# Layer 0's mixer of a two-layer hybrid network: small products put in another order, a low-rank factor split 80 + 80

## The chip, the cores and the metric

The kernel runs on one core of a Trainium2 chip. The metric is the device time of one execution in microseconds (us), the median of several runs. It is a forward pass of two layers over 256 tokens of width 2048, batch 1.

## The reference

Each layer is a mixer, a residual with a layer norm, a feed-forward block with a short convolution, and another residual with a layer norm. Layer 0's mixer, which the change touches, projects the tokens with one matrix, gives half of the columns to stick-breaking attention and the other half to a recurrence of 16 heads of 64:

```
rw = token_shift(rw, shift_mu)
r, kr, vr, dw, da, dg = split_last(rw, [1024, 1024, 1024, 64, 64, 160])
w_log = -softplus(-(w0 + tanh(dw) @ w2)) - 0.5
decay = exp(-exp(w_log))
a = sigmoid(a0 + da @ a2)
g = sigmoid(dg) @ g2                       # rank 160
kk = (k * k_k) per head, divided by its norm
k = k * (1 + (a - 1) * k_a)
state = state * w_t + (state @ -kk_t) (kk_t a_t)^T + v_t k_t^T     # per token and head
y = state @ r_t
out = (group_norm(y) + bonus) * g
```

Layer 1's mixer is gated linear attention; it is not touched.

## The kernel before, in words

**The large products.** All weights stream from HBM once. A *granule* is 128 x 512 weights in float32; ScalarE copies it into a rounded float32r part (L56), VectorE forms the remainder (L57), and TensorE makes three products for each operand pair, high by high, high by low and low by high (L185 to L187 for feature tiles, 12 products of 256 columns a granule; L195 to L197 for token tiles). These products take most of the time.

**What sets the order.** TensorE's order is the order in which the program is written; the other engines are ordered by a scheduler. Work beside the large products is written as generators (`spawn`): each `yield n` lets n granules pass (`tick`), then its next step is written into the stream. The names below are such generators of `Mix0.run`.

- `lora` (L588 and on): the low-rank steps. For each of 8 pairs of heads it makes two products, L601 for the decay (rows 0 to 63 of the low-rank input) and L602 for `a` (rows 64 to 127), of 256 columns in float32. ScalarE applies a sigmoid to each result (L157), VectorE sums the decays within chunks (L611). Pairs 0 to 3 are written in one batch, then a granule, then pairs 4 to 7, then a granule. Then ScalarE changes its table (L148) and raises the sums to exponents, two for each pair (L157, with a copy, L625). A granule later come the products of the gate, L634 with the first 128 of the 160 rows of `g2` and L635 with the last 32, four pairs, a granule, four pairs; VectorE copies them out (L636). `lw`, `g2a` and `g2b` lie in the three buffers through which the weights also arrive.
- `k_post` and `r_post`: for each pair the norm of the keys (L665 and ScalarE's logarithm and exponents), the scaled keys and queries (`BK` in `PB`, and `AR`, L678 to L690), and then the **Gram products**, L697: keys against queries for each of the 4 chunks of 64 tokens and each of the 2 heads. A head lies in 64 of the 128 partitions, so each product has 64 rows. The four chunks of the first head come first, then those of the second; each head has its own PSUM tile `pg`.
- `chain`: the recurrence over 4 chunks, for all 16 heads, in four steps a chunk that lie 4 granules apart: L809 (`pu`), L819 (`psa`), then L828 (`pS_`, the new state) and directly behind it the output `py`. `py` is the sum of two products per head: L840 from `SV` and `Gr` (128 rows, 64 columns of output) and, from chunk 1 on, L842 from the old state `So` and `AR` (64 rows). The two are written in turn, head by head: 16 + 16 products a chunk. `epilogue` then normalizes `py`.

A float32 product of the program shows as two MATMUL records, each with a weight load. The records name the shape: `128*64` is 128 rows by 64 output columns of the array, and `64x64` the partitions and columns of what streams.

PSUM tiles of these generators come from one pool of four (`t`).

Of the kernel before, what the change touches and what calls it, by code (L numbers as in the profile page):

```python
# [10 lines left out]
P = 128  # L11
S = 256
# [6 lines left out]
# how many granules the steps of the work beside the products lie apart  # L19
# [3 lines left out]
class Stream:  # L23
    """Weight granules [128, 512] in the order of use, split into two float32r parts."""
# [7 lines left out]
    def ahead(self):  # L32
        """split the first four granules before those of the stream before have been used"""
        K = self.K
        K.wpos = 0
        self.ready = [self.make() for _ in K.wbase]
# [27 lines left out]
class Kern:  # L64
# [14 lines left out]
    # Work beside the products: a generator that yields the number of granules to let pass  # L79
    # before its next step.  # L80
# [40 lines left out]
    def wpools(self, ctx, n, nraw, nw):  # L121
        """weights arrive n granules at a time"""
# [5 lines left out]
    def wextra(self, ctx, n, start=0):  # L128
        """room for n more granules as long as ctx is open"""
# [6 lines left out]
    def rsqrt(self, x, y, t):  # L136
        """y = x^-1/2 by exp(-ln(x)/2) and one step of Newton; t is scratch"""
        nc = self.nc
# [6 lines left out]
    # The table sets of ScalarE are loaded where act_set says: what needs a table is issued  # L145
    # behind its load, and a load behind what needs the set before it.
# [23 lines left out]
    def split(self, dst, src, eng_hi="act"):  # L170
        """dst [128, 2, n] float32r <- src in two parts"""
        nc = self.nc
# [6 lines left out]
    # out[f, tok] += W[k, f] x[k, tok]; a granule holds 4 k tiles of one feature tile  # L179
# [10 lines left out]
    # out[tok, n] += x[k, tok] W[k, n], both in two float32r parts; a granule holds 512 columns  # L190
    # of one k tile
# [7 lines left out]
    # out[tok, n] += x[k, tok] W[k, n]; a granule holds 512 columns of one k tile  # L199
    def wave(self, st, xT, made=None, first=False):  # L200
        """four feature tiles at once, k outside; made: steps that give 2 k tiles each"""
# [45 lines left out]
    def block_a(self, st, xs):  # L247
        """512 columns, both halves of the tokens"""
# [9 lines left out]
    def proj_out(self, xs, st, done, then=None, tail=4, after=None):  # L258
        """xs: (high, low) halves per k tile and token half; done(m, nb, ps, columns)"""
        nc = self.nc  # L260
        n = len(xs)
        for nb in range(4):
# [5 lines left out]
            # the first half of the tokens ends ahead of the second, and that in two parts  # L268
# [64 lines left out]
    def norm_out(self, h, g_d, b_d, out):  # L333
        """the last norm: a job before the sums are complete, that gives what follows each half"""
# [4 lines left out]
        # the blocks of each half that ScalarE and GpSimd take  # L339
# [164 lines left out]
C = 64  # L504
# [26 lines left out]
class Mix0:  # L531
# [19 lines left out]
    def run(self, xT, made, win_b, win_v, win_qk, lw_d, g2_d, open_h, outer):  # L551
# [6 lines left out]
        with ExitStack() as ctx:  # L558
# [28 lines left out]
            def lora(ps):  # L587
# [10 lines left out]
                for p in range(NP):  # L598
# [15 lines left out]
                    if p == 3:  # L614
                        yield 1
# [787 lines left out]
```

## Time and profile before

| | |
|---|---|
| median of three runs | 2439.29 us (2438.54 to 2439.73) |
| span of the profiled execution, first to last instruction | 2437.5 us |
| TensorE busy | 2405.3 us (99%) |
| VectorE busy | 1554.8 us (64%) |
| ScalarE busy | 1301.8 us (53%) |
| read from HBM | 429.77 MB, 177 GB/s over the span |
| mean granted TensorE clock | 0.991 |

The profiled execution's own time is its span, 2437.5 us; the median of the runs is 1.8 us above it, 0.07%. How to read a timeline row: start in us, length in us, engine, source line, operation, tiles written and read, shape, number of records merged, and in brackets the idle time of the engine ahead of it with what ended it. The lengths of TensorE's records overlap, so the time that a block takes is read from its first start to the start of what follows.

### The profile page before, as it was taken

The page shows a single profiled execution, that of the slowest core. Times are in us where ns is not written, and L with a number is a line of the kernel's source. Part 1 is how long each engine was busy: PE and PEld are TensorE (multiplying, and loading weights), DVE is VectorE, ACT ScalarE, POOL GpSimd, SP SyncE. Part 2 cuts the span into 40 slices and gives each one's busy share as a digit, 9 for nine tenths or more (in the row PEclk, how much of TensorE's full clock was granted, in tenths as well). Part 3 has the DMA queues.
Part 4 walks back from the last instruction along what each step waited for, and adds up shares of the span by engine and source line. Part 5 has one row for each costly group of instructions (what it writes and reads, how often), then busy time and mean ns, then how long its engine had stood idle before and what let it go on. Part 6 is the DMA issues. An engine that isn't in the chain of part 4 may idle for free.

```text
span 2437.5 us, 44745 instructions
## 1 busy us (share of the span) xinstructions
PE 2405.3 (99%) x17770; PEld 2253.8 (92%) x17770; DVE 1554.8 (64%) x2847; ACT 1301.8 (53%) x2450; POOL 12.0 (0%) x14
## 2 busy tenths in 40 slices
PE   8999999999999999999999999999999999999997
PEld 7998988889999999988898998989999999998887
DVE  5887755677666666655558666667766666655555
ACT  6655555555555555544437555555555555554442
POOL 0000000000000000000000000000000000000001
PEclk9999998999999999999999999999999999999999
DMA  5444433656555555555555554564655555565553
GB/s 175 161 134 168 145 105 104 210 163 224 189 184 185 188 183 188 184 193 195 184 173 177 170 173 166 175 213 163 218 184 189 183 185 188 183 216 199 195 186 138
DMA packets 123698, 434.79 MB, mean 178 GB/s; under 512 B 13744, under 2 KB 14640, under 8 KB 123488
## 3 DMA queue, kind: packets, MB, share of 16 engines
q1 hardware_dynamic: 123488, 431.93, 52.7%
q8 instruction: 139, 2.28, 0.4%
q14 instruction: 71, 0.58, 0.1%
HBM read 429.77 MB, written 2.10 MB: 177 GB/s over the span
## 4 chain that ended last, share of the span: by engine, by line
PE 95%; DVE 3%; DMA 1%; ACT 1%; issue 0%; SPq 0%; DVEq 0%; ACTq 0%
PE g L185 17%; PE g L187 17%; PE g L186 17%; PE g L195 10%; PE g L196 10%; PE g L197 10%; PE t L197 1%; PE t L195 1%; PE t L196 1%; DMA raw<-w0b 1%; PE g L213 1%; PE g L216 1%; PE g L214 1%; PE t L185 1%; PE t L187 1%; PE t L186 1%
## 5 line engine op out<-in xcount | busy, mean ns | idle before, releaser
L57 DVE TENSOR_TENSOR w<-raw,w 128x512 fp32r<-128x512 f32 x1584 | 1080.1, 690 | 769.9 <-ACT w L56 766.4
L56 ACT CAST w<-raw 128x512 fp32r<-128x512 f32 x1584 | 965.6, 620 | 958.3 <-PE g L187 461.4
L185 PE MATMUL g<-x,w 128*128 128x256 f32 x3024 | 852.6, 282 | 0.0
L187 PE MATMUL g<-x,w 128*128 128x256 f32 x3024 | 852.1, 282 | 0.0
L186 PE MATMUL g<-x,w 128*128 128x256 f32 x3024 | 851.8, 282 | 0.0
L185 PEld LDWEIGHTS g<-x,w 128*128 128x128 f32 x3024 | 569.7, 188 | 0.2
L186 PEld LDWEIGHTS g<-x,w 128*128 128x128 f32 x3024 | 569.7, 188 | 0.3
L187 PEld LDWEIGHTS g<-x,w 128*128 128x128 f32 x3024 | 569.6, 188 | 0.0
L197 PE MATMUL g<-w,hT 128*128 128x512 f32 (+1 forms) x704 | 255.4, 363 | 0.0
L196 PE MATMUL g<-w,hT 128*128 128x512 f32 (+1 forms) x704 | 255.3, 363 | 0.0
L195 PE MATMUL g<-w,hT 128*128 128x512 f32 (+1 forms) x704 | 255.3, 363 | 0.0
L185 PE MATMUL g<-xi,w 128*128 128x256 f32 x608 | 179.2, 295 | 0.0
L187 PE MATMUL g<-xi,w 128*128 128x256 f32 x608 | 173.4, 285 | 3.0 <-DVE w L57 2.9
L186 PE MATMUL g<-xi,w 128*128 128x256 f32 x608 | 172.8, 284 | 0.0
L195 PEld LDWEIGHTS g<-w,hT 128*128 128x128 f32 x704 | 133.0, 189 | 20.7
L196 PEld LDWEIGHTS g<-w,hT 128*128 128x128 f32 x704 | 133.0, 189 | 20.5
L197 PEld LDWEIGHTS g<-w,hT 128*128 128x128 f32 x704 | 132.9, 189 | 20.5
L187 PEld LDWEIGHTS g<-xi,w 128*128 128x128 f32 x608 | 116.1, 191 | 3.8 <-DVE w L57 3.8
L185 PEld LDWEIGHTS g<-xi,w 128*128 128x128 f32 x608 | 116.2, 191 | 3.1 <-issue 1.5
L186 PEld LDWEIGHTS g<-xi,w 128*128 128x128 f32 x608 | 116.3, 191 | 0.8
L213 PE MATMUL g<-x,w 128*128 128x256 f32 x192 | 55.8, 298 | 0.0
L157 ACT ACTIVATE ct<-ct 128x256 f32<-128x256 f32 x88 | 36.8, 418 | 32.5 <-DVE ct L457 32.5
(316 smaller groups left out, 2852.2 us busy)
## 6 DMA issues: line engine op xcount, KB each, us to landing
raw<-up SPq DMA_DIRECT2D x352, 512.0 KB, 3.6
raw<-dn SPq DMA_DIRECT2D x176, 512.0 KB, 4.3
raw<-w0b SPq DMA_DIRECT2D x53, 512.0 KB, 3.6
raw<-w1b SPq DMA_DIRECT2D x40, 512.0 KB, 3.8
raw<-w0qk SPq DMA_DIRECT2D x32, 512.0 KB, 3.6
raw<-w0o SPq DMA_DIRECT2D x32, 512.0 KB, 4.2
raw<-w1v SPq DMA_DIRECT2D x32, 512.0 KB, 3.6
raw<-w1o SPq DMA_DIRECT2D x32, 512.0 KB, 4.4
```

The costliest lines, as they stand in the source:

```text
L56: i = nc.scalar.copy(out=w[:, 0], in_=src).ins
L57: K.split_ins = nc.vector.tensor_sub(out=w[:, 1], in0=src, in1=w[:, 0].bitcast(F32)).ins
L157: i = self.nc.scalar.activation(out=out, in_=in_, func=func, **kw).ins
L185: nc.tensor.matmul(ps, lhsT=wh, rhs=xT[k][:, 0], start=k == 0, stop=False)
L186: nc.tensor.matmul(ps, lhsT=wh, rhs=xT[k][:, 1], start=False, stop=False)
L187: nc.tensor.matmul(ps, lhsT=wl, rhs=xT[k][:, 0], start=False, stop=k == KT - 1)
L195: nc.tensor.matmul(ps, lhsT=xh, rhs=w[0], start=first, stop=False)
L196: nc.tensor.matmul(ps, lhsT=xh, rhs=w[1], start=False, stop=False)
L197: nc.tensor.matmul(ps, lhsT=xl, rhs=w[0], start=False, stop=last)
L213: nc.tensor.matmul(ps[a], lhsT=wh, rhs=xT[k][:, 0], start=k == 0, stop=False)
L214: nc.tensor.matmul(ps[a], lhsT=wl, rhs=xT[k][:, 0], start=False, stop=False)
L216: nc.tensor.matmul(ps[a], lhsT=wh, rhs=xT[k][:, 1], start=False, stop=k == KT - 1)
```

## The change

Four edits, all in `Mix0`; comments were taken out besides, which moves line numbers by a few lines.

1. The output `py`: all 16 products of `SV` and `Gr` first, then all 16 of the old state. The first product of each half opens the accumulation of its PSUM region.
2. The Gram products of the two heads in turn, chunk by chunk, with both PSUM tiles taken ahead.
3. The 160 columns of the gate's low-rank input lie in two tiles of 80 and 80 in place of 128 and 32, and `g2` in two tiles of 80 rows.
4. `lora` writes two pairs, then lets a granule pass, four times, in place of four pairs twice. The exponents and the products of the gate thereby stand two granules later.

```diff
-    t = [(6144, 6272), (6272, 6400), (6400, 6432), k[0], k[1]]
+    t = [(6144, 6272), (6272, 6352), (6352, 6432), k[0], k[1]]
...
-                    if p == 3:
+                    if p % 2:
                         yield 1
-                yield 1
                 K.act_set("natural_log_exp_and_others")
...
-                nc.sync.dma_start(out=g2a, in_=g2_d[0:P])
+                nc.sync.dma_start(out=g2a[0:80], in_=g2_d[0:80])
...
-                nc.sync.dma_start(out=g2b[0:32], in_=g2_d[P:P + 32])
+                nc.sync.dma_start(out=g2b[0:80], in_=g2_d[80:160])
...
-                    nc.tensor.matmul(pw, lhsT=g2a[:, cs], rhs=l1, start=True, stop=False)
-                    nc.tensor.matmul(pw, lhsT=g2b[0:32, cs], rhs=l2[0:32], start=False, stop=True)
+                    nc.tensor.matmul(pw, lhsT=g2a[0:80, cs], rhs=l1[0:80], start=True, stop=False)
+                    nc.tensor.matmul(pw, lhsT=g2b[0:80, cs], rhs=l2[0:80], start=False, stop=True)
...
+                pgs = [K.t((P, NC_, P)) for _ in range(2)]
+                for c in range(NC_):
+                    for hh in range(2):
+                        q = slice(hh * 64, hh * 64 + 64)
+                        nc.tensor.matmul(pgs[hh][:, c], lhsT=BK[q, c].rearrange("p a b -> p (a b)"), rhs=AR[c // 2][q, c % 2, p], start=True, stop=True)
                 for hh in range(2):
-                    q = slice(hh * 64, hh * 64 + 64)
-                    pg = K.t((P, NC_, P))
-                    for c in range(NC_):
-                        nc.tensor.matmul(pg[:, c], lhsT=BK[q, c].rearrange("p a b -> p (a b)"), rhs=AR[c // 2][q, c % 2, p], start=True, stop=True)
+                    pg = pgs[hh]
...
                     for p in range(NP):
-                        b = p * NC_ + c
                         for hh in range(2):
                             q = slice(hh * 64, hh * 64 + 64)
-                            nc.tensor.matmul(py[q, p], lhsT=SV[:, p, c, hh], rhs=Gr[:, hh, b], start=True, stop=c == 0)
-                            if c:
-                                nc.tensor.matmul(py[q, p], lhsT=So[q, p], rhs=AR[c // 2][q, c % 2, p, C:P], start=False, stop=True)
+                            nc.tensor.matmul(py[q, p], lhsT=SV[:, p, c, hh], rhs=Gr[:, hh, p * NC_ + c], start=p == 0, stop=c == 0 and p == NP - 1)
+                    for p in range(NP if c else 0):
+                        for hh in range(2):
+                            q = slice(hh * 64, hh * 64 + 64)
+                            nc.tensor.matmul(py[q, p], lhsT=So[q, p], rhs=AR[c // 2][q, c % 2, p, C:P], start=False, stop=p == NP - 1)
```

TensorE, the state step and the output of chunk 1 in the kernel before (`t_4221` is the new state, `t_4241` is `py`); the row pair L840, L842 goes on to 32 rows:

```order
L187 MATMUL g_4156<-xi_99,w_4206 128x256
L828 MATMUL t_4221<-SV,BKT 64x64 x16
L840 MATMUL t_4241<-Gr,SV 64x64
L842 MATMUL t_4241<-AR_121,St_2014 64x64
L840 MATMUL t_4241<-Gr,SV 64x64
```

The same place in the changed kernel, where the three loops stand at L829, L841 and L845:

```order
L187 MATMUL g_4156<-xi_99,w_4206 128x256
L829 MATMUL t_4221<-SV,BKT 64x64 x16
L841 MATMUL t_4241<-Gr,SV 64x64 x16
L845 MATMUL t_4241<-AR_121,St_2014 64x64 x16
L185 MATMUL g_4280<-xi_84,w_4283 128x256
```

The products are the same 48; two shapes that stood in turn 32 times now stand in two runs, and the run of L841 follows L829, which has its shape.

TensorE, the Gram products of the first pair of heads in the kernel before (`t109` and `t110` are the PSUM tiles of the first and the second head):

```order
L697 MATMUL t109_908<-AR0_121,PB_123 128x128 x2
L697 MATMUL t109_908<-AR1_122,PB_123 128x128 x2
L697 MATMUL t110_915<-AR0_121,PB_123 128x128 x2
L697 MATMUL t110_915<-AR1_122,PB_123 128x128 x2
L707 MATMUL t111_925<-e93_794,ct_79 128x256
```

And in the changed kernel:

```order
L696 MATMUL t109_908<-AR0_121,PB_123 128x128
L696 MATMUL t110_909<-AR0_121,PB_123 128x128
L696 MATMUL t109_908<-AR0_121,PB_123 128x128
L696 MATMUL t110_909<-AR0_121,PB_123 128x128
L696 MATMUL t109_908<-AR1_122,PB_123 128x128
L696 MATMUL t110_909<-AR1_122,PB_123 128x128
L696 MATMUL t109_908<-AR1_122,PB_123 128x128
L696 MATMUL t110_909<-AR1_122,PB_123 128x128
L708 MATMUL t111_925<-e89_778,ct_79 128x256
```

The second head's products moved between those of the first; nothing else moved there.

ScalarE, the last exponents of `lora` (`E6`, `E7`), the weight casts and the first step of the key norm of pair 0 (L157 into `e73` before, `e61` in the change) in the kernel before:

```order
L157 ACTIVATE E7_631<-E7_631 128x256
L157 ACTIVATE E6_617<-E6_617 128x260
L157 ACTIVATE E7_631<-E7_631 128x260
L625 COPY eE_128<-E6_617 128x4
L625 COPY eE_128<-E7_631 128x4
L56 CAST w96_803<-raw95_801 128x512
L56 CAST w97_818<-raw95_801 128x512
L157 ACTIVATE e73_644<-e89_759 128x256
L157 ACTIVATE e73_644<-e73_644 128x256
```

And in the changed kernel:

```order
L157 ACTIVATE E7_669<-E7_669 128x256
L624 COPY eE_128<-E6_655 128x4
L157 ACTIVATE e61_588<-e81_727 128x256
L157 ACTIVATE E7_669<-E7_669 128x260
L56 CAST w99_835<-raw98_833 128x512
L56 CAST w103_870<-raw98_833 128x512
L624 COPY eE_128<-E7_669 128x4
L157 ACTIVATE e61_588<-e61_588 128x256
L141 ACTIVATE e82_728<-e61_588 128x256
```

All 16 exponents still stand ahead of the key norm's second step; the first moved between them, and the casts that stand there are those of two granules later.

## Rows read from the trace of the kernel before

**Rows 1.** The page: the span, and the chain that ended last.
```profile
span 2437.5 us, 44745 instructions
...
PE 95%; DVE 3%; DMA 1%; ACT 1%; issue 0%; SPq 0%; DVEq 0%; ACTq 0%
```

**Rows 2.** Timeline, TensorE, output of chunks 1, 2 and 3: first rows and what follows.
```profile
348.60 0.28 PE L840 MATMUL t<-Gr,SV 128*64 128x64 f32 x2
...
358.25 0.58 PE L185 MATMUL g<-xi,w 128*128 128x256 f32 x1
...
383.50 0.28 PE L840 MATMUL t<-Gr,SV 128*64 128x64 f32 x2
...
393.59 0.58 PE L185 MATMUL g<-xi,w 128*128 128x256 f32 x1
...
418.23 0.33 PE L840 MATMUL t<-Gr,SV 128*64 128x64 f32 x2
...
428.78 0.79 PE L195 MATMUL g<-w,oS 128*128 128x512 f32 x1
```

**Rows 3.** Timeline, TensorE: output of chunk 0, which has L840 alone.
```profile
325.55 1.10 PE L840 MATMUL t<-Gr,SV 128*64 128x64 f32 x32
326.58 0.50 PE L195 MATMUL g<-w,xi 128*128 128x512 f32 x1
```

**Rows 4.** Timeline, TensorE: one L819 block, 64-row products of two heads in turn.
```profile
340.64 1.15 PE L819 MATMUL t<-Ga,XT 64*64 64x64 f32 x32
341.71 0.39 PE L185 MATMUL g<-xi,w 128*128 128x256 f32 x1
```

**Rows 5.** Windows, TensorE: stretch, length, busy (records), granted clock, DMA share, GB/s.
```profile
40.10:43.50 3.40, 3.40 (x16) 0.50 0.00 0
...
324.50:326.50 2.00, 2.00 (x65) 1.00 0.32 125
...
358.30:360.90 2.60, 2.60 (x13) 0.50 0.00 0
...
393.60:398.40 4.80, 4.80 (x21) 0.50 0.00 0
...
428.80:432.60 3.80, 3.80 (x12) 0.50 0.72 171
```

**Rows 6.** Timeline, TensorE: the low-rank products of both batches, and the granules behind each.
```profile
35.95 0.48 PE L601 MATMUL t<-e,lw 64*128 64x256 f32 x1 [0.63 <-ACT e L157]
...
36.27 0.38 PE L601 MATMUL t<-e,lw 64*128 64x256 f32 x1
...
36.49 0.59 PE L601 MATMUL t<-e,lw 64*128 64x256 f32 x2
37.45 0.70 PE L602 MATMUL t<-e,lw 64*128 64x256 f32 x2 [0.36 <-ACT e L157]
...
40.00 0.53 PE L185 MATMUL t<-xi,w 128*128 128x256 f32 x1
...
42.80 0.79 PE L601 MATMUL t<-e,lw 64*128 64x256 f32 x1
...
46.64 0.39 PE L185 MATMUL g<-xi,w 128*128 128x256 f32 x1
```

**Rows 7.** Timeline, TensorE: first batch of the gate's products, and what follows.
```profile
49.62 0.59 PE L634 MATMUL t<-e,g2a 128*128 128x256 f32 x2
...
54.53 0.39 PE L185 MATMUL g<-xi,w 128*128 128x256 f32 x1
```

**Rows 8.** Timeline, TensorE: Gram products of the first pair, and what follows.
```profile
71.32 1.71 PE L697 MATMUL t<-AR,PB 64*128 64x128 f32 x16 [0.28 <-DVE AR L690]
72.96 0.70 PE L707 MATMUL t<-e,ct 128*128 128x256 f32 x2
```

**Rows 9.** Waits in 34 to 75 us: who waited for whom, total, times, longest.
```profile
ACT e L157 <- DVE e L668: 4.1, 1, 4.1
```

**Rows 10.** Windows, 75 to 168 us: length; PE, PEld, DVE, ACT, POOL busy; clock, DMA.
```profile
75.00:168.00 93.00, 93.00 (x770) 90.61 (x768) 80.73 (x200) 56.57 (x122) 1.81 (x1) 1.00 0.43 144
```

More of the change, by code (lines that the diff above doesn't have):

```diff
@@ L524, in mix0_mu_cols @@
 def mix0_mu_cols():
-    t = [(6144, 6272), (6272, 6400), (6400, 6432)]
+    t = [(6144, 6272), (6272, 6352), (6352, 6432)]
     for o in (1024, 0, 2048):
```

## The prediction, made blind

> **What bounds the kernel now.** I read the page first: TensorE carries 95% of the chain that ended last, in a span of 2437.5 us [rows 1]. So time that TensorE no longer spends in its queue comes off the end, as long as no other engine is late in its place. Then I went through the timeline of TensorE over layer 0's mixer, block by block, each from its first start to the start of what follows, and through the windows for the granted clock. The reader is to see two things. The small products differ many times over in what one record takes: 32 records of L840 alone take 1.03 us in chunk 0 [rows 3], while 64 records of L840 and L842 in turn take 9.65, 10.09 and 10.55 us in chunks 1 to 3 [rows 2], 0.15 to 0.16 us a record against 0.032. And behind those slow blocks the clock stands at 0.50, the 1.2 GHz level, for a while after the large products have resumed [rows 5]. The sum is made against the profiled execution, 2437.5 us; the median of the runs shown, 2439.29, is 1.8 above, and I take the gain off that.
>
> **The state chain (edit 1).** Nothing is added or removed; the 64 records of each of three chunks stand in two runs. The first run is what chunk 0 already does: 1.03 us [rows 3]. The second, 64 rows by 64 columns with the two heads in opposite corners of the array, has no row of its own; the nearest is L819, the same shape with the same alternation of heads: 32 records from 340.64 to 341.71, 1.07 us [rows 4]. Between the runs the shape changes once. A price for that comes from the gate's products, which change from 128 to 32 rows and back: 4.91 us for 16 records in 8 groups of two, 0.61 a group [rows 7], where two records of one row group and of the same width follow each other at 0.22 (36.27 to 36.49) [rows 6], so 0.44 a group; the difference is 0.17 us a change. The change of shape between L828 and L840 doesn't exist: both are 128 by 64. So a block becomes 1.03 + 1.07 + 0.17 = 2.27 us, three are 6.8 in place of 9.65 + 10.09 + 10.55 = 30.3, and the gain is **23.5 us**. Ends: 0 if the turn-taking is not what costs, 24 if the change of shape is free. I take the value near the upper end, since rows 3 and 4 are the same kind of block in the same stage.
>
> Rows 4 show 64-row products of two heads, with both results in one PSUM tile, at 33 ns a record. The Trainium skill (TensorEngine Tiling (Array Packing), "Restrictions and Gotchas") says that different row tiles cannot access the same PSUM bank at the same time. By that rule the two heads of L842, which write one `py` tile, would go one after the other. The rows speak against it here, as L819 writes its two heads into one tile too; what the sum would be with such a queue is worked out below from the rows.
>
> **The clock behind the chain.** Large products ran at 0.50 for 2.6, 4.8 and 3.8 us directly behind the three blocks [rows 5]. The same work at 1.00 takes half, a gain of **5.6 us** if the clock stays up. Ahead of each fall TensorE had done nothing but slow small records since the block began; ahead of 326.5, where L828 and 32 records of L840 ran 2 us at their quick pace, it stayed at 1.00 [rows 5]. The new burst, with L828, is about 3.3 us. Ends: 0 and 5.6; I take 5.6, as the burst is nearer to the one without a fall.
>
> **The low-rank steps (edit 4).** Before, the two batches take 35.95 to 40.00 and 42.80 to 46.64, together 7.89 us [rows 6]. Their first pair is quick, four records to 36.49, 0.54 us, the two row halves side by side; then L602 waits for ScalarE's sigmoid to free a PSUM tile (37.45), and the batch goes on at ScalarE's pace [rows 6]. With four tiles in the pool and four wanted per batch, two pairs should find room and go at 0.54 a pair: 4 x 1.08 = 4.3 us; I add 0.1 a batch for tiles that the key norm holds, 4.7. Gain 3.2. The granule between the batches ran at half clock, 40.00 to 42.80, 2.80 us, where the two behind the second batch take 46.64 to 49.62, 1.49 each [rows 5 to 7]; with short batches the clock should hold, gain 1.3. Together **4.5 us**. Ends: 0 (ScalarE sets the pace anyhow) and 5.7 (four records in 0.44, no waits).
>
> **The gate's products (edit 3).** 16 + 16 products as before, each on 80 rows. If 80 rows run as 128 do, there is no change of shape: 32 records at 0.22 are 7.0 us in place of twice 4.91 (the second batch is as long as the first), gain **2.8 us**. No row shows 80 rows; the other end is 0, that 80 rows next to 80 cost what 128 next to 32 do. I take the upper, since both halves now have one shape. The sigmoid on 128 partitions, the count of granules and of DMAs stay, and the two tiles of `g2` are still one DMA each: nothing there.
>
> **The Gram products (edit 2).** A block takes 71.32 to 72.96, 1.64 us [rows 8]. Side by side the two heads need 8 steps in place of 16. A step of two 64-column records is 1.07 / 16 = 0.067 us [rows 4]; of 128 columns twice that, 0.134: 1.07, and 0.1 for the start, 1.17. Gain 0.47 for each of 8 pairs, **3.7 us**. Ends: 0, and 6.1 if a step takes 0.11, half of the 256-column record's 0.22.
>
> **What will be late next.** The exponents stand two granules later, and VectorE and ScalarE get less time. At the first Gram block VectorE is already the last to come, by 0.28 us [rows 8]. With the numbers above TensorE arrives there 4.5 + 2.8 = 7.3 us earlier. The last low-rank batch ends at 35.95 + 4.7 + 3 x 1.49 = 45.1 in place of 46.64, so ScalarE can change its table 1.5 earlier; and ScalarE's wait of 4.1 us for the key norm [rows 9] disappears, since that product now stands ahead of the gate's. The chain to the first Gram block thus ends some 5.6 us earlier against TensorE's 7.3: a new wait of about 2 us with the 0.28. Behind the waiting products stand all large ones, so it counts fully. From 75 to 168 VectorE is busy 80.73 of 93 us [rows 10]; with 3.7 less it is at 90%, so I give back 0.5. In the chain each epilogue must follow one granule behind a `py` that ends sooner, 0.3 for each of three, 1.0. Together **-3.5 us**, with ends of 0 and -8. SP's queue keeps its order but for one weight transfer ahead of `g2`; it hides behind the granules that use it.
>
> **Sum.** 23.5 + 5.6 + 4.5 + 2.8 + 3.7 - 3.5 = 36.6 us, 1.5%: a span of 2400.9 and a time of 2402.7.
>
> **The rivals.** *ScalarE and VectorE take the place of TensorE ahead of 75 us.* For it: the 0.28 already there, VectorE's 87%. Against: the idle 4.1 us. Then edits 3 and 4 give nothing, 7.3 less: 2410. *The clock still falls behind the chain*: 5.6 are lost and about 2 more inside the blocks: 2410; against it the 2 us burst without a fall. *The two row halves queue for one PSUM tile*: each L842 run takes twice 1.07, 3.2 us less gain: 2406; rows 4 speak against it. It is how things would go by the rule of the Trainium skill named above. *The reorder does not do what it says*: the price lies in adding onto a PSUM region and not in the turn-taking. Then the chain and its clock give nothing, 29.1 less: 2432; the gate's products, which take turns with a price of their own, speak against it. *Slower:* the quick small records keep the clock at its 1.2 GHz level. Place: the chain stage from 324 to 450 us, some 95 us of work after the change. At the half level each microsecond of work costs one more, so if all of it ran so the time would be near 2498; it is slower than before from 37 us of such work on. Against it: before the change the level returned within 2.6 to 4.8 us of large products [rows 5].
>
> **How the numbers follow.** Forecast 0.74, late ScalarE and VectorE 0.13, falling clock 0.05, queue for the PSUM tile 0.03, reorder without effect 0.03 (two thirds of it lands near no change with the new waits), half clock throughout 0.02. A measurement of this kernel can tell about 0.2%, 4.9 us, from no change. Faster by more: 0.96; within: 0.02; slower: 0.02. The range reaches down to the better ends of edits 2 and 4 without new waits, 2396, and up past the two rivals at 2410, to 2412; it leaves out the last two rivals and the tails.
>
> **What would show it.** The `py` blocks of chunks 1 to 3 at 2.2 to 2.4 us each and a clock of 1.00 behind them; Gram blocks near 1.2; four low-rank batches near 1.1 to 1.2; gate batches near 3.5; an idle of TensorE of about 2 us ahead of the first Gram block, ended by VectorE or by the weights queued behind it. The prediction is wrong if a `py` block stays above 4 us, if the clock is at 0.50 between 345 and 430, or if TensorE gathers more than 8 us of new idle time ahead of 170 us.

## The result, and the profile after

The changed kernel takes **2410.67 us**, the median of four runs (2409.47 to 2412.84); the kernel before took 2439.51 in its four (2438.54 to 2442.56). The ratio is 0.988, with a 95% interval of 0.9866 to 0.9894. The gain is 28.8 us where 36.6 were forecast; the time lies inside the range and 8.0 us above the predicted one.

| | before | after |
|---|---|---|
| span of the profiled execution | 2437.5 us | 2411.0 us |
| TensorE busy | 2405.3 us | 2376.0 us |
| VectorE busy | 1554.8 us | 1553.2 us |
| ScalarE busy | 1301.8 us | 1301.8 us |

The page of the changed kernel: the chain that ended last, as in [rows 1].

```profile
PE 94%; DVE 3%; DMA 1%; ACT 1%; issue 0%; SPq 0%; DVEq 0%; ACTq 0%
```

TensorE still sets the end, so what its queue loses comes off. The timeline of TensorE in the changed kernel shows the output of chunks 1 and 3 (columns as in [rows 2]; L841 was L840, L845 was L842):

```profile
344.95 1.10 PE L841 MATMUL t<-Gr,SV 128*64 128x64 f32 x32
345.98 1.15 PE L845 MATMUL t<-AR,St 64*64 64x64 f32 x32
347.06 0.39 PE L185 MATMUL g<-xi,w 128*128 128x256 f32 x1
...
396.12 1.15 PE L841 MATMUL t<-Gr,SV 128*64 128x64 f32 x32
...
398.28 0.50 PE L195 MATMUL g<-w,oS 128*128 128x512 f32 x1
```

Each of the three blocks is 2.11 or 2.16 us from start to follower, where it was 9.65 to 10.55 [rows 2]. The windows over and behind the three blocks (columns as in [rows 10]) have the clock at 1.00 throughout, where it stood at 0.50 for 2.6 to 4.8 us [rows 5]; the last row is a place where it falls now and did not before:

```profile
344.90:348.50 3.60, 3.60 (x84) 3.46 (x81) 2.94 (x5) 1.27 (x3) 0.00 (x0) 1.00 0.54 192
371.10:374.60 3.50, 3.50 (x81) 3.37 (x78) 2.10 (x6) 2.68 (x6) 0.00 (x0) 1.00 0.30 84
396.10:399.60 3.50, 3.50 (x71) 3.12 (x71) 1.33 (x3) 2.00 (x4) 0.00 (x0) 1.00 0.57 208
174.10:180.90 6.80, 6.13 (x27) 5.45 (x28) 4.83 (x16) 2.19 (x6) 0.00 (x0) 0.50 0.42 154
```

The other small products of the changed kernel, on the same timeline: first low-rank batch and what follows each of the first two, a batch of the gate, and the Gram products of the first two pairs (answering to [rows 6 to 8]). The last row is a wait at a place that is called the transposes below: there VectorE makes four transposes (L746, 2 us each) that open an inverse which the recurrence needs.

```profile
36.40 0.48 PE L601 MATMUL t<-e,lw 64*128 64x256 f32 x1 [0.40 <-ACT e L157]
...
38.96 0.70 PE L602 MATMUL t<-e,lw 64*128 64x256 f32 x2 [1.43 <-ACT e L157]
39.59 0.39 PE L185 MATMUL t<-xi,w 128*128 128x256 f32 x1
...
41.22 0.48 PE L601 MATMUL t<-e,lw 64*128 64x256 f32 x1
...
43.10 0.39 PE L185 MATMUL g<-xi,w 128*128 128x256 f32 x1
...
51.84 0.60 PE L633 MATMUL t<-e,g2a 80*128 80x256 f32 x2
52.27 0.59 PE L634 MATMUL t<-e,g2b 80*128 80x256 f32 x2
...
55.11 0.47 PE L185 MATMUL g<-xi,w 128*128 128x256 f32 x1
...
67.27 1.16 PE L696 MATMUL t<-AR,PB 64*128 64x128 f32 x16
68.36 0.70 PE L708 MATMUL t<-e,ct 128*128 128x256 f32 x2
...
81.23 0.71 PE L696 MATMUL t<-AR,PB 64*128 64x128 f32 x8
82.12 0.72 PE L696 MATMUL t<-AR,PB 64*128 64x128 f32 x8 [0.17 <-DVE AR L689]
84.11 0.67 PE L708 MATMUL t<-e,ct 128*128 128x256 f32 x2 [1.27 <-DVE e L690]
...
174.77 0.87 PE L724 MATMUL t<-ct,e 128*128 128x128 f32 x3 [2.96 <-DVE e L752]
```

The same place in the kernel before:

```profile
181.09 0.52 PE L723 MATMUL t<-ct,e 128*128 128x128 f32 x3 [2.51 <-DVE e L751]
```

The reader is to see three gains and three waits. A gate batch is 3.27 us (4.91 before), a Gram block 1.09 (1.64). But the first low-rank batch takes 3.19 for two pairs, with a wait of 1.43 for ScalarE; the Gram products of the second pair and the product behind them wait 0.17 + 1.27 for VectorE; and L724 waits 2.96, where its predecessor L723 waited 2.51.

To say where time went, all kernels are cut at the same large products. Each has 16266 of them (L185 to L187, L195 to L197, L213 to L216) in the same order, so the start of the n-th (counted from 0), read from each trace, is a common mark. Lengths in us of the stretches that differ, one profiled execution each (the runs follow below):

| kernel | first L601 to product 300 (low-rank, gate) | 300 to 972 (Gram) | 972 to 1068 (transposes) | 1900 to 2264 (chain) | 2700 to 6500 |
|---|---|---|---|---|---|
| before | 28.4 | 104.0 | 16.6 | 95.8 | 453.9 |
| after | 23.6 | 101.6 | 19.8 | 67.5 | 459.0 |
| e1_py_only | 26.9 | 104.1 | 16.6 | 67.4 | 454.6 |
| e2_rest_only | 25.4 | 101.6 | 18.4 | 95.8 | 454.0 |
| e3_after_again | 26.9 | 101.6 | 18.5 | 67.5 | 454.0 |
| e4_turn_no_add | 26.9 | 104.1 | 16.6 | 96.0 | 454.0 |
| e5_pairs | 25.3 | 101.8 | 19.8 | 73.1 | 453.9 |
| e6_key_tile | 20.7 | 103.9 | 18.6 | 67.5 | 454.4 |
| e7_spread | 23.5 | 102.0 | 19.9 | 67.4 | 454.0 |
| e8_three | 20.7 | 103.1 | 18.8 | 67.4 | 454.2 |
| e9_spread_held | 23.7 | 101.5 | 14.4 | 67.4 | 454.9 |
| e10_no_edit4 | 23.8 | 102.9 | 17.1 | 67.4 | 454.4 |
| e11_best | 23.8 | 102.5 | 14.4 | 67.5 | 454.8 |
| e12_no_edit2 | 27.7 | 106.0 | 16.6 | 67.4 | 454.7 |

From before to after the columns give +4.8, +2.4, -3.2, +28.3 and -5.1. The first L601 starts 0.45 later, product 2264 to 2700 gains 0.7, and what lies behind product 6500 loses 1.15. Together 26.4, the difference of the two spans. The first stretch of e6 and e8 is short because their first L601 starts 3.8 and 4.9 later than the change's, behind a wait told below.

### The profile page after: what moved, and what is told of

It is laid out like the page before. It is cut to its first block, busy times and chain, and to the rows that moved or that the text cites. A ratio compares the mean times of both kernels' runs of the same rounds, so it can differ in the third digit from the quotient of the medians.

```text
span 2411.0 us, 44746 instructions
## 1 busy us (share of the span) xinstructions
PE 2376.0 (99%) x17770; PEld 2236.0 (93%) x17770; DVE 1553.2 (64%) x2847; ACT 1301.8 (54%) x2450; POOL 12.0 (0%) x14
## 4 chain that ended last, share of the span: by engine, by line
PE 94%; DVE 3%; DMA 1%; ACT 1%; issue 0%; SPq 0%; DVEq 0%; ACTq 0%
PE g L185 17%; PE g L187 17%; PE g L186 17%; PE g L195 10%; PE g L197 10%; PE g L196 10%; DMA raw<-w0b 1%; PE t L197 1%; PE t L196 1%; PE t L195 1%; PE g L213 1%; PE g L214 1%; PE g L216 1%; DVE w L57 1%; PE t L185 1%; PE t L187 1%
## 5 line engine op out<-in xcount | busy, mean ns | idle before, releaser
L57 DVE TENSOR_TENSOR w<-raw,w 128x512 fp32r<-128x512 f32 x1584 | 1079.1, 690 | 777.9 <-ACT w L56 774.2
L185 PE MATMUL g<-x,w 128*128 128x256 f32 x3024 | 856.4, 283 | 0.0
L187 PE MATMUL g<-x,w 128*128 128x256 f32 x3024 | 855.1, 283 | 0.0
L185 PEld LDWEIGHTS g<-x,w 128*128 128x128 f32 x3024 | 570.6, 189 | 0.2
L187 PEld LDWEIGHTS g<-x,w 128*128 128x128 f32 x3024 | 569.2, 188 | 0.0
L197 PE MATMUL g<-w,hT 128*128 128x512 f32 (+1 forms) x704 | 255.2, 363 | 0.0
L195 PE MATMUL g<-w,hT 128*128 128x512 f32 (+1 forms) x704 | 255.2, 363 | 0.0
L185 PE MATMUL g<-xi,w 128*128 128x256 f32 x608 | 178.9, 294 | 0.1
L187 PE MATMUL g<-xi,w 128*128 128x256 f32 x608 | 172.6, 284 | 3.1 <-DVE w L57 3.1
L195 PEld LDWEIGHTS g<-w,hT 128*128 128x128 f32 x704 | 132.9, 189 | 20.6
L197 PEld LDWEIGHTS g<-w,hT 128*128 128x128 f32 x704 | 132.9, 189 | 20.6
L187 PEld LDWEIGHTS g<-xi,w 128*128 128x128 f32 x608 | 115.5, 190 | 3.9 <-DVE w L57 3.9
L185 PEld LDWEIGHTS g<-xi,w 128*128 128x128 f32 x608 | 115.6, 190 | 3.8 <-issue 2.4
L213 PE MATMUL g<-x,w 128*128 128x256 f32 x192 | 55.8, 298 | 0.0
L157 ACT ACTIVATE ct<-ct 128x256 f32<-128x256 f32 x88 | 36.8, 418 | 32.7 <-DVE ct L457 32.6
```

The lines of the kernel that those rows point to most:

```text
L57: K.split_ins = nc.vector.tensor_sub(out=w[:, 1], in0=src, in1=w[:, 0].bitcast(F32)).ins
L157: i = self.nc.scalar.activation(out=out, in_=in_, func=func, **kw).ins
L185: nc.tensor.matmul(ps, lhsT=wh, rhs=xT[k][:, 0], start=k == 0, stop=False)
L187: nc.tensor.matmul(ps, lhsT=wl, rhs=xT[k][:, 0], start=False, stop=k == KT - 1)
L195: nc.tensor.matmul(ps, lhsT=xh, rhs=w[0], start=first, stop=False)
L197: nc.tensor.matmul(ps, lhsT=xl, rhs=w[0], start=False, stop=last)
```

## The experiments

**The `py` edit alone** (before, with edit 1):

```diff
-                            nc.tensor.matmul(py[q, p], lhsT=SV[:, p, c, hh], rhs=Gr[:, hh, b], start=True, stop=c == 0)
-                            if c:
-                                nc.tensor.matmul(py[q, p], lhsT=So[q, p], rhs=AR[c // 2][q, c % 2, p, C:P], start=False, stop=True)
+                            nc.tensor.matmul(py[q, p], lhsT=SV[:, p, c, hh], rhs=Gr[:, hh, p * NC_ + c], start=p == 0, stop=c == 0 and p == NP - 1)
+                    for p in range(NP if c else 0):
+                        for hh in range(2):
+                            q = slice(hh * 64, hh * 64 + 64)
+                            nc.tensor.matmul(py[q, p], lhsT=So[q, p], rhs=AR[c // 2][q, c % 2, p, C:P], start=False, stop=p == NP - 1)
```

> The kernel before with edit 1 alone, the two runs of py products. If edit 1 carries the gain of the chain, the blocks of chunks 1 to 3 take 2.1 us each in place of 9.7 to 10.6 and the clock stays at 1.00 behind them: 28.3 us less up to 450 us, a time near 2411. The rival, that the chain gained because edits 2 to 4 shifted the work against the clock, gives blocks above 4 us or a clock at 0.50 behind them.

Measured: 2412.21 us (2411.03 to 2418.65) against 2440.16 of before, ratio 0.9891 (0.9876 to 0.9906). The chain takes 67.4 us, 28.4 less; the granted clock does not fall anywhere ahead of 496 us. Edit 1 alone is nearly the whole result.

**All but that edit** (the diff above, the other way round, in the changed kernel):

> The changed kernel with edit 1 undone: edits 2, 3 and 4 alone. By the changed kernel's own trace they give 3.65 us up to 320 us, with a fall of the clock at 174 us that may or may not come again: a time of 2432 to 2437. By my forecast of these edits (4.5 + 2.8 + 3.7 less 2.5) it would be 2431.

Measured: 2436.57 us (2433.57 to 2441.07, ten runs) against 2440.16, ratio 0.9981 (0.997 to 0.9992). Edits 2 to 4 together give 3.6 us, where the forecast had 11.0 less new waits of 2.5 for them. With e1's 27.95 the two make 31.5, 2.7 more than the change measures; its own four runs lie 3.4 apart.

**The change again**, beside those two:

> The changed kernel once more, for what is its own and what belongs to one execution. If the slower rhythm of the large products between 520 and 990 us (120.0 ns a product against 118.7) and the clock at 0.50 from 174 to 181 us are set by the order of the program, both come again. If they are of one execution, at least one is gone, and the span is up to 8 us shorter.

Measured: 2412.01 us (2407.98 to 2415.72), ratio 0.9884 (0.987 to 0.9899). The windows of this execution show the clock down among the low-rank steps, which the other execution of the same kernel doesn't have (36.4 to 49.0 at 1.00), and the stretch behind the chain at the pace of before. So the slower rhythm of the large products is gone; the half clock at the transposes came again, for 3.4 us from 179.9 on, behind a wait of 2.94.

```profile
43.30:50.10 6.80, 6.80 (x28) 5.09 (x26) 3.61 (x13) 3.64 (x8) 0.00 (x0) 0.50 0.15 48
550.00:650.00 100.00, 100.00 (x845) 100.00 (x844) 66.42 (x117) 54.04 (x101) 0.00 (x0) 1.00 0.62 202
```

So two executions of one kernel differ by 3 to 5 us in single stretches, and stretches tell more here than totals. Where a time stands below without a range, it is of one execution; the eight of the change itself lie between 2407.98 and 2415.72.

**Taking turns without adding.** Before, with the product of the old state written to a PSUM tile of its own; the output lacks that part.

```diff
+                    po = K.t((P, NP, C))
...
-                                nc.tensor.matmul(py[q, p], lhsT=So[q, p], rhs=AR[c // 2][q, c % 2, p, C:P], start=False, stop=True)
+                                nc.tensor.matmul(po[q, p], lhsT=So[q, p], rhs=AR[c // 2][q, c % 2, p, C:P], start=True, stop=True)
```

> The kernel before, with the old state's products L842 in turn as they were but written to a PSUM tile of their own and not added: the output lacks that part. If turns between shapes are what costs, blocks stay at 9.6 to 10.6 us. If adding onto a PSUM region is, they fall to 2.1 to 2.5 us.

Measured: 2437.73 us, chunk 1 on TensorE's timeline (the last rows stand at half clock):

```profile
347.54 0.28 PE L841 MATMUL t<-Gr,SV 128*64 128x64 f32 x2
347.75 0.32 PE L843 MATMUL t<-AR,St 64*64 64x64 f32 x2
348.00 0.33 PE L841 MATMUL t<-Gr,SV 128*64 128x64 f32 x2
...
356.91 0.47 PE L843 MATMUL t<-AR,St 64*64 64x64 f32 x2
357.32 0.58 PE L185 MATMUL g<-xi,w 128*128 128x256 f32 x1
```

Nothing is added onto a region, and the block still takes 347.54 to 357.32, 9.78 us. The turn-taking is the price, and the rival "adding onto a PSUM region" falls.

**Half as many turns**: pair by pair, both heads of one shape, then both of the other.

```diff
-                            nc.tensor.matmul(py[q, p], lhsT=SV[:, p, c, hh], rhs=Gr[:, hh, p * NC_ + c], start=p == 0, stop=c == 0 and p == NP - 1)
-                    for p in range(NP if c else 0):
-                        for hh in range(2):
+                            nc.tensor.matmul(py[q, p], lhsT=SV[:, p, c, hh], rhs=Gr[:, hh, p * NC_ + c], start=True, stop=c == 0)
+                        for hh in range(2 if c else 0):
```

> The changed kernel with the two products of py in turn pair by pair: both heads of L840's kind, then both of L842's, 16 changes of shape a chunk in place of 32 or 1. If each change costs a fixed time on top and two heads of one shape run side by side, a group of two program products takes about what a single one took, 0.26 us, and a block 16 x 0.26 = 4.1 us at full clock. If only the full run is quick, blocks stay near 8 us or more.

Measured: 2414.94 us. Chunk 1 on TensorE's timeline:

```profile
346.82 0.29 PE L840 MATMUL t<-Gr,SV 128*64 128x64 f32 x4
347.04 0.33 PE L843 MATMUL t<-AR,St 64*64 64x64 f32 x4
347.30 0.34 PE L840 MATMUL t<-Gr,SV 128*64 128x64 f32 x4
...
350.99 0.39 PE L185 MATMUL g<-xi,w 128*128 128x256 f32 x1
```

A group of four records takes 0.26 us, the same as a group of two at full clock in e2 and e4 (0.25 to 0.26). The block takes 4.17, twice the two straight runs. The starts of the single records say why. In a run of one shape the records of the two heads start side by side, 0.007 us apart, and each such step of two records is 0.058 us behind the one before. At the one change of shape in the changed kernel (chunk 1, the last two records of L841 and the first two of L845):

```profile
345.82 0.23 PE L841 MATMUL t<-Gr,SV 128*64 128x64 f32 x2
345.98 0.27 PE L845 MATMUL t<-AR,St 64*64 64x64 f32 x2
```

The step to L845 takes 0.158, the next one 0.107, where two steps of a run take 0.117: a change of shape costs 0.14 to 0.15 us. In e5 a group is two steps and a change, 0.117 + 0.147 = 0.264. In e4 and before it is also two steps and a change, for half the records: head by head, the two records of a product follow each other at 0.058 and the other head doesn't run beside them. So a block of before pays twice, for 32 changes and for twice as many steps. An estimate from these numbers: at full clock it would take 32 x 0.257 = 8.2 us, 6.1 more than the two straight runs, 4.2 of it by 30 more changes and 1.9 by 32 more steps. The rest of its 9.65 to 10.55, some 5.6 for the three blocks, is half clock inside the block. The Trainium skill (TensorEngine Tiling (Array Packing), "Key Properties") says that changing the tiling mode drains the engine; these rows agree, and give the drain a size. The clock stays at 1.00 behind these blocks of 4.2 us.

**The key product of the second pair out of the small pool.** Of the pool's four PSUM tiles one is held, during the first two low-rank batches, by the product of pair 1's keys (`t` in L185 at 39.59 above). Here that product takes a tile of the large products' pool.

```diff
-            k_in(1, tile_b(K.t))
+            k_in(1, tile_b())
```

> The changed kernel with the key product of pair 1 in the PSUM pool of the large products, so that the low-rank steps find all four tiles of their own pool free. If the tile that this product held is what made the first two batches slow (3.2 to 3.8 and 1.9 to 2.9 us), all four batches now take 1.07 to 1.2 us, the wait of 1.4 to 2.0 us for ScalarE in the first is gone, and the clock does not fall there. If ScalarE's sigmoids set the pace, the waits move to batches 2 to 4 and the sum of the four stays above 6 us.

Measured: 2410.03 us. TensorE's timeline:

```profile
34.20 0.39 PE L185 MATMUL g<-xi,w 128*128 128x256 f32 x1 [3.05 <-DVE e L549]
...
40.18 0.48 PE L601 MATMUL t<-e,lw 64*128 64x256 f32 x1
...
41.24 0.39 PE L185 MATMUL g<-xi,w 128*128 128x256 f32 x1
...
52.68 0.59 PE L633 MATMUL t<-e,g2a 80*128 80x256 f32 x2
```

All four batches now take 1.07 us, as forecast for edit 4. But TensorE waits 3.05 ahead of them, in the key product, for VectorE to read out a tile of the other pool; the clock stands at 0.50 behind that, from 34.8 to 38.2, and the gate's products start at 52.68, after 51.84 in the change. The wait moved: freeing the held tile speeds up the batches and gains nothing.

**The transposes two granules apart** (`yield 2` for `yield 1` ahead of each, and the inverse's steps a little closer):

> The changed kernel with the four transposes that open the inverse two granules apart in place of one (three later steps of the inverse one granule closer, so that it ends when it did). If the wait of 2.9 us at 175 to 180 us and the half clock behind it come from VectorE's 8 us of transposes in a row, the wait falls below 1 us and the clock stays at 1.00; the stretch between the products 972 and 1068 of the stream takes 15 us or less in place of 18.5 to 19.8 (16.6 before the change). If VectorE is simply full there, the wait moves and the stretch stays above 17 us.

Measured: 2409.77 us, wait 2.94 as in the change. The scheduler left VectorE's order as it was, two transposes back to back, so this run does not test what it meant to.

**Three at once**: e6, e7, and the product for the bonus (L708) two granules later.

> Both of these, and the bonus product (L708) written two granules later, behind the wait of 1.3 us that it has for VectorE with pair 1. If the three waits are what edits 2 to 4 gave back, some 2.9 + 3 + 1.4 us come off: 2404 to 2406, against 2411 of the changed kernel. If TensorE waits elsewhere for VectorE instead, the time stays at 2409 or more.

Measured: 2410.39 us (2408.51 to 2412.68), ratio 0.986 (0.9835 to 0.9886). Waits of 3.25 (at 35.3), 2.17 (at 85.3, now L696 itself for VectorE's L689) and 2.92 (at 178.5): each moved or stayed, and no time came off.

**The transposes held apart.** Each is tied behind the latest split of a weight granule.

```diff
-                        yield 1
+                        yield 3
...
-                    nc.vector.transpose(out=M[q * 32:q * 32 + 32], in_=Ga[q * 32:q * 32 + 32, q // 2, :, o:o + 32].rearrange("p b t -> p t b"))
+                    i = nc.vector.transpose(out=M[q * 32:q * 32 + 32], in_=Ga[q * 32:q * 32 + 32, q // 2, :, o:o + 32].rearrange("p b t -> p t b"))
+                    if q:
+                        K.behind(i.ins, K.split_ins)
...
-                        yield 2 if 4 <= i < 28 else 1
+                        yield 2 if 4 <= i < 22 else 1
```

> The four transposes of VectorE stand apart here, with weight splits between them, in place of two that stand back to back. If their order makes the wait of TensorE at about 175 us (2.96 us in the change, 2.51 us before), that wait falls under 1 us, the granted clock stays at 1.00 behind it, and the stretch from the 972nd to the 1068th product of that stage takes 15 to 17 us instead of 19.8; the kernel is 3 to 4 us shorter than the change. If VectorE is simply full from the Gram products on, the wait stays at 2 us or more or comes back at another tile, the stretch stays over 18 us, and the time is the change's within 1.5 us.

Measured: 2403.46 us, span 2401.6. VectorE's timeline in the change:

```profile
168.89 4.01 DVE L746 STREAM_TRANSPOSE INV<-Ga 32x1024 f32<-32x1024 f32 x2
172.93 1.29 DVE L57 TENSOR_TENSOR w<-raw,w 128x512 fp32r<-128x512 f32 x2
174.14 0.48 DVE L549 SCALAR_TENSOR_TENSOR e<-g,vec,e 128x255 f32<-128x255 f32 x1
```

in this kernel:

```profile
169.28 2.04 DVE L746 STREAM_TRANSPOSE INV<-Ga 32x1024 f32<-32x1024 f32 x1
171.35 0.69 DVE L57 TENSOR_TENSOR w<-raw,w 128x512 fp32r<-128x512 f32 x1
171.97 0.48 DVE L549 SCALAR_TENSOR_TENSOR e<-g,vec,e 128x255 f32<-128x255 f32 x1
...
174.53 2.06 DVE L746 STREAM_TRANSPOSE INV<-Ga 32x1024 f32<-32x1024 f32 x1
```

TensorE's product that takes what L549 makes (the shifted values), in this kernel:

```profile
172.50 0.55 PE L724 MATMUL t<-ct,e 128*128 128x128 f32 x3 [0.29 <-DVE e L549]
```

and its window behind that (columns as in [rows 10]):

```profile
173.00:180.00 7.00, 7.00 (x58) 6.51 (x56) 6.94 (x13) 3.99 (x10) 0.00 (x0) 1.00 0.55 178
```

L549 and two splits (L57) stood behind two transposes of 2.0 us each; with one of these behind them L549 comes 2.2 us sooner, the wait falls from 2.96 to 0.29 and the clock stays at 1.00. The profile puts the wait in the change down to L752, but L724 reads the shifted values that L549 writes (end 174.62), and nothing of L752. VectorE is as full as it was (6.94 of 7.00 us in the window): it was the order, not the amount. The stretch takes 14.4 us, 5.4 less than in the change and 2.2 less than before.

**Without edit 4** (the change with one batch of four pairs twice):

```diff
-                    if p % 2:
+                    if p == 3:
                         yield 1
+                yield 1
```

> The change with its low-rank steps of one pair at a time again (edits 1 to 3 alone). If edit 4 gives nothing, the stretch from the first low-rank product to the 300th product of the stage takes 23.3 to 23.9 us, as in the change (23.6 us), or about 1.5 us more where the granted clock falls in it, and the kernel takes the change's time within 1.5 us. If edit 4 gives the 4.5 us of the forecast, the stretch takes 27 to 28 us and the kernel is 4 to 5 us longer than the change.

Measured: 2406.66 us, span 2404.9. The first stretch takes 23.8 us, as with edit 4 (23.6). The first Gram block, though, waits here, where the change has no wait (timeline of TensorE):

```profile
68.75 1.16 PE L697 MATMUL t<-AR,PB 64*128 64x128 f32 x16 [1.52 <-DVE AR L690]
...
176.11 0.52 PE L725 MATMUL t<-ct,e 128*128 128x128 f32 x3 [2.96 <-DVE e L753]
```

The window at the transposes:

```profile
174.00:181.00 7.00, 4.89 (x39) 4.55 (x40) 6.83 (x20) 2.82 (x7) 0.00 (x0) 1.00 0.41 150
```

The span is 6.1 us below the change's in spite of that, from two things: the clock did not fall at the transposes (1.00, behind the same wait of 2.96 as in the change; 17.1 us for that stretch against 19.8), and the stretch 2700 to 6500 went 4.6 faster. The second belongs to the change's one execution. The first may be edit 4's: in all seven executions that have edits 2 and 4 and the transposes back to back (the change, e2, e3, e5, e6, e7, e8) the clock fell there, behind waits of 2.92 to 2.96, and here it did not; one execution without edit 4 can't settle it. So the total is a miss for both theories, and the stretches answer: edit 4 gives nothing in the low-rank steps, and 1.3 us behind them. From the first L601 to product 1068 the change takes 144.9 us (146.9 in e3) and this kernel 143.7, so with the transposes as they are no gain of edit 4 shows.

**Both** (edits 1 to 3, the transposes held apart):

> Edits 1 to 3 of the change with the transposes held apart. If edit 4 gives nothing and the order of the transposes makes the wait at about 175 us, this takes 2405 to 2409 us, 2 to 6 us less than the change's 2410.7. If VectorE is full there whatever the order, it takes the change's time within 1.5 us; if edit 4 was worth its 4.5 us, it takes 2411 to 2416 us.

Measured: **2402.28 us** (2400.68 to 2404.18, five runs) against 2444.31 of before on that chip, ratio 0.983 (0.981 to 0.9849). The interval lies below the change's, so this version beats both kernels. The expectation's lower bound was missed by 2.7 us, as the transposes give 5.4 and not 3 to 4. Beside e9, the same kernel with edit 4 and on the same chip, it shows what that edit does once the transposes are apart: the stretches to product 1068 add up, from the first L601, to 139.7 in e9 and 140.7 here. Edit 4 gives about 1 us there, by the first Gram block (a wait of 1.32 here, none in e9). The times as a whole don't tell the two apart: e9's 2403.46 lies among the five here. How it makes that block's input earlier was not traced.

**Without edit 2** (edits 1, 3 and 4):

```diff
-                pgs = [K.t((P, NC_, P)) for _ in range(2)]
-                for c in range(NC_):
-                    for hh in range(2):
-                        q = slice(hh * 64, hh * 64 + 64)
-                        nc.tensor.matmul(pgs[hh][:, c], lhsT=BK[q, c].rearrange("p a b -> p (a b)"), rhs=AR[c // 2][q, c % 2, p], start=True, stop=True)
                 for hh in range(2):
-                    pg = pgs[hh]
+                    q = slice(hh * 64, hh * 64 + 64)
+                    pg = K.t((P, NC_, P))
+                    for c in range(NC_):
+                        nc.tensor.matmul(pg[:, c], lhsT=BK[q, c].rearrange("p a b -> p (a b)"), rhs=AR[c // 2][q, c % 2, p], start=True, stop=True)
```

> The change without its edit 2: the Gram products of the first head, then those of the second, as before (edits 1, 3 and 4 alone). If the turn-taking is worth its 0.54 us in each of 8 blocks, the stretch from the 300th product (behind the gate's products) to the 972nd (ahead of the transposes), 116.4 us in the change, takes 120 to 121 us. Two theories part at the transposes: if VectorE is what is late there and TensorE only arrives earlier by edit 2, the wait at about 178 us shrinks from 2.96 to under 1 us, most of the 4.3 us is taken back, and the kernel is within 2 us of the change; if the wait stays at 2.5 to 3 us, VectorE is shifted along with TensorE, edit 2 keeps its gain, and the kernel is 4 to 5 us longer than the change, 2414 to 2416 us.

Measured: 2414.24 us. TensorE's first Gram block and its wait at the transposes:

```profile
72.06 1.71 PE L696 MATMUL t<-AR,PB 64*128 64x128 f32 x16
73.69 0.70 PE L706 MATMUL t<-e,ct 128*128 128x256 f32 x2
...
183.38 0.52 PE L722 MATMUL t<-ct,e 128*128 128x128 f32 x3 [2.51 <-DVE e L750]
```

and VectorE's first three transposes:

```profile
171.59 4.00 DVE L744 STREAM_TRANSPOSE INV<-Ga 32x1024 f32<-32x1024 f32 x2
...
176.95 2.03 DVE L744 STREAM_TRANSPOSE INV<-Ga 32x1024 f32<-32x1024 f32 x1
```

From product 300 to 972 it takes 106.0 us, 4.4 more than the change: edit 2 gives that much, most of it as 0.54 in each of seven blocks (the second pair's has the waits shown above). The waits in this stretch add up to much the same, 1.67 in the change and 1.80 here. The wait at the transposes is again the 2.51 of before, with the order of before (the two adjoining transposes first), and no fall of the clock. So edit 2 changes VectorE's order there. Of its 4.4 us 3.2 are lost again in the change, 0.45 as a longer wait and 2.7 as clock (19.8 against e10's 17.1). The longer wait is edit 2's, as e10 has it too; the clock fell only where edits 2 and 4 stood together. The span, 2412.4, lies 1.4 above the change's: 4.4 for edit 2 and 4.1 for the first stretch (the clock stood at 0.50 for 10.2 us from 39.0 on), less the 3.2 at the transposes and the 4.3 between products 2700 and 6500 that the change lost there.

## Why the prediction was right or wrong

- **The state chain and the clock behind it: right.** Forecast 23.5 + 5.6 - 1.0 = 28.1, measured 28.3 in the change and 28.4 alone. The blocks gave 23.9. They take 2.11 and not 2.27, as the price of the change of shape was counted twice: the 1.03 of [rows 3] and the 1.07 of [rows 4] run up to the next shape's first record and hold it already. The large products behind them gave 4.4 and not 5.6. But by the estimate at e5 some 5.6 of the 23.9 were half clock inside the blocks, so the clock makes some 10 of the 28.3 and the turn-taking some 18; the prediction had put the whole of the blocks down to turn-taking. The 1.0 for the epilogues was not needed: no wait stands there.
- **Queue for one PSUM tile: refuted.** L845's two row halves write one `py` tile, and 32 records take 1.08 us, not twice that. The "Restrictions and Gotchas" of the page TensorEngine Tiling (Array Packing) of the Trainium skill would have them wait for each other; the measurement decides against it for these two halves.
- **The gate (edit 3): right.** 2 x (4.91 - 3.27) = 3.3 against 2.8. 80 rows run at 0.43 a group of two, 0.22 a record, the pace of the 64-row records in [rows 6].
- **The Gram products (edit 2): the block right, what follows it wrong.** 1.09 to 1.12 in seven of the eight blocks against 1.17, 4.4 in all against 3.7. That VectorE had other work in another order at the end of that stage did not stand in the sum.
- **The low-rank steps (edit 4): this step failed.** "With four tiles in the pool and four wanted per batch, two pairs should find room": one tile was held by the key product, for which I had added 0.1 a batch. The first batch took 3.19 and the second 1.88. With the tile freed (e6) all four take 1.07, and the same time is waited elsewhere; so the limit lies in the engines that feed and empty these tiles (ScalarE in the change, VectorE in e6) and not in TensorE; it is near the lower end that the prediction gave (0, ScalarE's pace). The batches add up to 7.2 us in place of 7.89, and e10 shows no loss without the edit. "With short batches the clock should hold" is also refuted: with edit 4 it fell ahead of 52 us in e2, e5, e6, e8 (3.4 us each), e3 (6.8) and e12 (10.2) and not in the change's first execution, e7 and e9; without edit 4 it fell in before (3.4) and not in e1, e4, e10 and e11. The edit does not keep it up. About 1 us came instead at the first Gram block, and with the transposes as they are even that doesn't show. What makes the time of the low-rank steps the same with and without the edit was not traced further.
- **What will be late next: the place was wrong.** The 2 us forecast ahead of the first Gram block did not come with edit 4 (it has no wait; 1.3 to 1.5 without). The waits came at the second pair (0.17 + 1.27) and at the transposes (0.45 more, and 2.7 of clock); together 4.6 against 3.5. That the price was near is luck, as the waits are others. The stretch from 75 to 168 was looked at for its busy share only: VectorE was 89% busy there (83.13 of 93 after, forecast 90%), and what cost was the order of a handful of its instructions just behind that stretch.
- **The rival** that ScalarE and VectorE take TensorE's place ahead of 75 us was half right: edit 4's gain went that way and edit 3's did not. Its total, 2410, is the measured one, but by other terms.
- **The remainder.** Of the 10.2 us by which the two profiled spans fall short of the forecast gain, 5.1 lie between products 2700 and 6500, which no edit touches and no other run here shows. They belong to that one execution, the slowest of its four; whether one of the untraced ones has them too isn't known, so they can't be put into the 8.0 by which the median falls short. Of those 8.0 the term of edit 4 makes some 4.5.

## What to carry to other kernels

Write small products of different tile shape in runs of one shape: here a change of shape cost 0.14 to 0.15 us, taking turns head by head also kept two heads from running side by side, and the clock's fall in and behind such slow blocks came on top. Before counting a gain on the bounding engine, read what the others have queued at the next place where it waits for them, instruction by instruction: a transpose of 2 us ahead of a short operation cost more than the busy share could tell. Where a wait goes when a buffer is freed is to be tried before it is counted; here it moved to another pool.

## What the runs showed of the hardware

The large products go in one of two rhythms. Behind the chain, 100 us of them hold 845 records (118.7 ns from start to start over the stretch) in before, in e3 (window above) and in every other run; in the first profiled execution of the change they held 835 (120.0 ns) from 520 to 986 us, at the same granted clock, which cost the 5.1 us. Its window:

```profile
550.00:650.00 100.00, 100.00 (x835) 100.00 (x835) 65.05 (x114) 54.36 (x100) 0.00 (x0) 1.00 0.58 194
```

What makes it take the one or the other stays open.

The granted clock fell behind a wait of 2.9 us at the transposes in the change (6.8 us at 0.50), in e3 (3.4) and in e2, e5, e6, e7 and e8 (3.4 or 6.8), and did not behind the same wait in e10, nor behind the 2.51 or 2.52 of before, e1, e4 and e12. The length of a wait alone does not tell whether the level falls.

It fell without any wait inside all nine blocks of before, e2 and e4 in which the two shapes take turns product by product, and in none of the three blocks of e5, which take 4.2 us.
